# Gated delta net: a level's two independent tiled products in one burst, and tiled steps of two heads side by side

## The chip, the cores and the metric

The kernel runs on one core of a Trainium2 chip. The metric is the device time of one execution in microseconds (us); the kernel before is given by the median of three runs. The engines are PE (TensorE, matrix products), DVE (VectorE), ACT (ScalarE), POOL (GpSimd) and SP (SyncE, which issues transfers).

## The reference

A stack of four blocks over a sequence of 512 tokens of width 1024, in float32: a first block with a pooling mixer and a gated delta net, an MLP, a sparse attention block and a state space block. The change is in the gated delta net of the first block. It has 4 heads of width 128; the sequence is cut into 8 chunks of 64 tokens. Per head and chunk it computes

```python
kb = kh * beta[..., None]
m = jnp.einsum('bhncd,bhnjd->bhncj', kb, kh) * decay_strict
lhs = jnp.eye(C, dtype=f32) + m
rhs = jnp.concatenate([vh * beta[..., None], kb * jnp.exp(gcum)[..., None]], axis=-1)
sol = lax.linalg.triangular_solve(lhs, rhs, left_side=True, lower=True)
value, k_cumdecay = sol[..., :Dh], sol[..., Dh:]
attn_inner = jnp.einsum('bhncd,bhnjd->bhncj', qh, kh) * decay_incl
...
v_new = val - jnp.einsum('bhcd,bhde->bhce', kc, state)
o = jnp.einsum('bhcd,bhde->bhce', qd, state) + jnp.einsum('bhcj,bhje->bhce', ai, v_new)
state = state * jnp.exp(gl)[..., None, None] + jnp.einsum('bhcd,bhce->bhde', kd, v_new)
```

The step that matters here is the inverse of the 64x64 unit lower triangular `lhs`.

## The kernel before

**Two streams on PE.** In the first block PE has a main stream: dense products of 128x128 weights with 512 tokens, each float32 product made of three float32r matmuls (line 133, called L133 in the profile). They are the projections of `w_in` (20 tiles of 24 matmuls: keys, queries and values of heads 0 to 3, gates, pooling) and then `w_out`. Beside it run side streams, each a Python generator: `gdn_chain` for each head, `gdn_norm` behind it, `decays` once, `pooling` four times. A chain starts when its head's three convolutions are there and the head before it has passed level 4 (`mid`), so the end of one head overlaps with the start of the next: this text calls it a hand-over, of which there are three.

**The planner.** `weave` writes the order on PE. It keeps a clock `t` in estimated us. One step of the main stream is one dense matmul and counts 0.22. A side stream yields a pair after each step: what the step cost, and how long until its next step may run; the second figure is multiplied by `LATE` = 1.1. The side step with the earliest due time runs when it is due and nothing is owed; after a side step of cost c the main stream is owed 0.5 c, paid by dense matmuls. PE and SP follow this order to the letter (`manual_schedule(engines=MANUAL)`); DVE, ACT and POOL are ordered by the scheduler of the language, by priority (`RUSH` for side steps) and by what is ready in its model.

**The chain of a head.** Its products by line: `pk` (514, four transposes of the keys, from which POOL makes the squares `ksq` and DVE the norms `k2`, `rk2`, `brk2` and later `rk`), `pq` and `pn` (533 to 536, keys times keys and queries, the array split into two tiles of 128x64), `pd` (539, 540, decays), then six levels, 0 to 5, that build the inverse by doubling, then the join of two chunks (639 to 648), then `pz`, `pA`, `pc`, `po` and the pass over the states (`pS`, lines 685 to 691).

A level works on eight 64x64 matrices, four on partitions 0 to 63 and four on 64 to 127; a helper `each` issues eight products, each of which is two matmul instructions in the trace, on the array tiles at (0, 0) and (64, 64). These 64x64 products, and `pq` with `pn`, are called tiled here. Level n has
- `pb` (579): the level's mask of `M` (`Ms`, made by POOL) times `U`; ACT copies it to `B`.
- `px` (584, from level 2 on): the `B0` of the level before times `X`; DVE subtracts it from `X`.
- `pu` (588): `X` times `B`; DVE subtracts it from `U` (at level 5 into `UU`, line 595).

`px` does not depend on the `pb` of its level; `pu` needs both. Before the change the chain yields between each two of the three, so dense matmuls or another stream's steps stand between them. Behind level 1 there is a step `pv`, behind level 3 `pr`, behind level 4 `q2` (`token_sums`). The join at lines 639 and 640 issues a last `px` and a `pb` that reads `UU`, in one step already.

Banks of PSUM for the chain come from a pool of five.

Of the kernel before, what the change touches and what calls it, by code (L numbers as in the profile page):

```python
# [20 lines left out]
LATER = 4000  # L21
POOLED = (2, 3, 4, 5)
LATE = 1.1
SHARE = 0.5
BLOCKED = object()


def weave(tc, main, sides):

    t, owed, active = 0.0, 0.0, []
    while sides or active:
        for e in list(sides):
            if e[0]():
                sides.remove(e)
                active.append([t, e[1]])
        due = min(active, key=lambda e: e[0]) if active else None
        if due is None or due[0] > t or owed > 0.0:
            owed -= 0.22  # L40
            if next(main, BLOCKED) is BLOCKED:
                assert due is not None or any(e[0]() for e in sides)
                t, owed = max(t, due[0] if due else t), 0.0
            else:
                t += 0.22
            continue
        with tc.high_priority(RUSH):
            step = next(due[1], None)
        if step is None:
            active.remove(due)  # L50
        else:
            t += step[0]
            owed = max(owed, -0.22) + SHARE * step[0]
            due[0] = t + LATE * step[1]
    while next(main) is not BLOCKED:
        pass

# [10 lines left out]
class Kit:  # L68
# [217 lines left out]
    def bank(self):  # L286
        return self.norm_bank() if self.norm_bank else self.psd.tile([128, 512], F32, tag="ps", name="ps")
# [188 lines left out]
def gdn_chain(K, h, inputs, cst, G, gw, bank, result, mid):  # L476
# [14 lines left out]
    def bc(t, n):  # L491
        return t[:, :, None].to_broadcast([t.shape[0], 4, n])

    def each(f):
        for i in range(4):
            for x in range(2):
                f(i, halves[x], (x * 64, x * 64))

    def v4(t):
        return t.rearrange("p (i c) -> p i c", i=4)  # L500
# [23 lines left out]
    nc.vector.reciprocal(rk2, k2)  # L524
    brk2 = gw.tile([128, 4], F32, tag="brk2", name="brk2")
    nc.vector.tensor_tensor(brk2, rk2, beta, ALU.mult)
    yield 0.5, 0.0

    pq, pn = bank("pq"), bank("pn")
    for i in range(4):  # L530
# [29 lines left out]
    Mn = dec[:, 2]  # L560
    nc.vector.tensor_tensor(Mn[high], Mn[high], bc(brk2[high], 64), ALU.mult)
    nc.vector.tensor_tensor(Mn[high], v4(pn[high, 0:256]), Mn[high], ALU.mult)
    yield 0.9, 5.0


    foldb = fold[:, None, :].to_broadcast([128, 4, 64])
    for n in range(6):
        lev = cst[:, None, C_LEV + 64 * n:C_LEV + 64 * n + 64].to_broadcast([128, 4, 64])
        Ms = gw.tile([128, 4, 64], F32, tag="Ms", name="Ms", bufs=4)
        nc.gpsimd.tensor_tensor(Ms, M, lev, ALU.mult)  # L570
        pb = bank("pb")
        if n == 0:
            each(lambda i, s, tp: mm(pb[s, i * 64:i * 64 + 64], Ms[s, i, :], fold[s, :], start=True, stop=True, tile_position=tp))
            U, X = (gw.tile([128, 4, 64], F32, tag=t, name=t) for t in "UX")
            nc.vector.tensor_tensor(U, foldb, v4(pb[:, 0:256]), ALU.subtract)
            nc.gpsimd.tensor_tensor(X, foldb, Ms, ALU.subtract)
        else:
            B = gw.tile([128, 4, 64], F32, tag="B", name="B", bufs=3)
            each(lambda i, s, tp: mm(pb[s, i * 64:i * 64 + 64], Ms[s, i, :], U[s, i, :], start=True, stop=True, tile_position=tp))  # L579
            nc.scalar.copy(B, v4(pb[:, 0:256]))  # L580
            yield 0.6, 0.0
            if n > 1:
                px = bank("px")
                each(lambda i, s, tp: mm(px[s, i * 64:i * 64 + 64], B0[s, i, :], X[s, i, :], start=True, stop=True, tile_position=tp))
                nc.vector.tensor_tensor(X, X, v4(px[:, 0:256]), ALU.subtract)
                yield 0.6, 1.0
            pu = bank("pu")
            each(lambda i, s, tp: mm(pu[s, i * 64:i * 64 + 64], X[s, i, :], B[s, i, :], start=True, stop=True, tile_position=tp))
            if n < 5:
                nc.vector.tensor_tensor(U, U, v4(pu[:, 0:256]), ALU.subtract)  # L590
            else:
                UU = gw.tile([128, 4, 128], F32, tag="s2", name="UU", bufs=2)
                nc.gpsimd.memset(UU[high, :, 0:64], 0.0)
                for s in (high, low):
                    nc.vector.tensor_tensor(UU[s, :, s], U[s], v4(pu[s, 0:256]), ALU.subtract)
            B0 = B
        yield 0.6, 1.0
        if n == 1:

            pv = bank("pv")  # L600
            for i in range(4):
                nc.tensor.transpose(pv[:, i * 128:i * 128 + 128], vT[:, i * 128:i * 128 + 128], ident)
            rk = gw.tile([128, 4], F32, tag="rk", name="rk")
            K.rsqrt(rk, k2, "g")
            brke = gw.tile([128, 4], F32, tag="brke", name="brke")
            nc.vector.tensor_tensor(brke, brk2, eg, ALU.mult)
            brk = gw.tile([128, 4], F32, tag="brk", name="brk")
            nc.vector.tensor_tensor(brk, rk, beta, ALU.mult)
            R = gw.tile([128, 4, 256], F32, tag="R", name="R")
            nc.vector.tensor_tensor(R[:, :, 0:128], pv.rearrange("p (i d) -> p i d", i=4), bc(brk, 128), ALU.mult)  # L610
            nc.gpsimd.tensor_tensor(R[:, :, 128:256], kt, bc(brke, 128), ALU.mult)
            yield 0.5, 0.2
        if n == 2:
            kd = gw.tile([128, 4, 128], F32, tag="kd", name="kd")
            nc.gpsimd.tensor_tensor(kd, kt, bc(ekd, 128), ALU.mult)
        if n == 3:

            pr = bank("pr")
            for part, first in ((ghi, True), (glo, False)):
                d = gw.tile([128, 4, 128], F32R, tag="s2", name="gd", bufs=2)  # L620
                nc.gpsimd.tensor_tensor(d, ident[:, None, :].to_broadcast([128, 4, 128]), bc(part, 128), ALU.mult)
                mm(pr, G["ones"], d.rearrange("p i c -> p (i c)"), start=first, stop=not first)
            qc = gw.tile([128, 4, 128], F32, tag="kt", name="qc")
            qcf = qc.rearrange("p i c -> p (i c)")
            nc.scalar.activation(qcf, pr, AF.Exp)
            nc.gpsimd.tensor_tensor(qcf, qcf, kq[:, 1, :], ALU.mult)
            qq = gw.tile([128, 512], F32, tag="s2", name="gqq", bufs=2)
            nc.scalar.activation(qq, kq[:, 1, :], AF.Square)
            yield 0.9, 0.2
        if n == 4:  # L630
            mid.add(h)
            q2 = K.token_sums([(qq, K.ones[:, 0:1])], 128 * EPS, 128 * EPS * EPS, "gts", bank("pt"))
            yield 0.9, 0.0


    px, pb = bank("px"), bank("pb")
# [4 lines left out]
    nc.vector.tensor_tensor(X[low], X[low], v4(px[low, 0:256]), ALU.subtract)  # L641
    B = gw.tile([128, 4, 64], F32, tag="B", name="B", bufs=3)
    nc.scalar.copy(B[low], v4(pb[low, 0:256]))
    yield 0.6, 1.0
    pu = bank("pu")
    for i in range(4):
        mm(pu[low, i * 64:i * 64 + 64], X[low, i, :], B[low, i, :], start=True, stop=True, tile_position=(0, 0))
# [71 lines left out]
def block1(K, vec, wcol, W, V, mx, mixh, mixl, then):  # L719
# [5 lines left out]
    with tc.tile_pool(name="gq", bufs=1) as gq, tc.tile_pool(name="gw", bufs=2) as gw, \  # L725
# [209 lines left out]
        with tc.manual_schedule(engines=MANUAL):  # L935
            for done, ps in held:
                done(ps)
            sides.append((lambda: True, dc))
            for h in range(4):
                sides.append((lambda h=h: "gcum" in G and len(convs.get(h, ())) == 3 and (h < 2 or h - 2 in o) and (h < 1 or h - 1 in mid),  # L940
                              gdn_chain(K, h, inputs, cst, G, gw, bank, o, mid)))
                sides.append((lambda h=h: h in o and h in zs, gdn_norm(K, h, zs, o, V, gw, bank, mixh[4 + h], mixl[4 + h], mixed)))
            weave(tc, K.passes, sides)
# [27 lines left out]
def nsa(K, norms, W, cst, first, then):  # L971
# [12 lines left out]
    with ExitStack() as pools:  # L984
# [342 lines left out]
        def units():  # L1327
# [4 lines left out]
            for n in range(len(items) + LAGS[2]):  # L1332
                for stage, lag in enumerate(LAGS):
# [10 lines left out]
                    if n - lag < len(items):  # L1344
                        yield FILL[at[0]][at[1]] * 0.22 / SHARE / 3, 0.0

# [17 lines left out]
        with tc.manual_schedule(engines=MANUAL):  # L1364
            for c in range(2):
                p.memset(KD[c][:, :, 511:528], 0.0)
            p.memset(Vc, 0.0)
            K.norm_bank = lambda: bank("norm")
            K.lead(K.norm2_steps(*norms, R), R, held, 28, 42)
            K.norm_bank = None  # L1370
            weave(tc, K.passes, sides)
# [778 lines left out]
```

## Time and profile before

| | us |
|---|---|
| median of three runs | 1344.16 |
| lowest, highest | 1341.83, 1345.73 |
| profiled execution, its own time | 1345.95 |
| span of the profiled execution | 1343.8 |
| mean granted clock of TensorE in it | 0.983 |

The span runs from the first to the last instruction. The gated delta net lies between 40 and 260 us of it. A timeline row reads: start, length from the first start to the last end, engine, line, operation, output and inputs by the program's names, weight and operand shapes, count, and in brackets the idle time of the engine before it with its releaser. Matmuls overlap, so the pace is read from starts, not from lengths. A row of source gives minimum, median and maximum ns of one instruction, first and last start, and forms. A row of waits gives who waited for whom, us in total, times, and the longest. [...]

### The profile page before, as it was taken

The page shows a single profiled execution, that of the slowest core. Times are in us where ns is not written, and L with a number is a line of the kernel's source. Part 1 is how long each engine was busy: PE and PEld are TensorE (multiplying, and loading weights), DVE is VectorE, ACT ScalarE, POOL GpSimd, SP SyncE. Part 2 cuts the span into 40 slices and gives each one's busy share as a digit, 9 for nine tenths or more (in the row PEclk, how much of TensorE's full clock was granted, in tenths as well). Part 3 has the DMA queues.
Part 4 walks back from the last instruction along what each step waited for, and adds up shares of the span by engine and source line. Part 5 has one row for each costly group of instructions (what it writes and reads, how often), then busy time and mean ns, then how long its engine had stood idle before and what let it go on. Part 6 is the DMA issues. An engine that isn't in the chain of part 4 may idle for free.

```text
span 1343.8 us, 22524 instructions
## 1 busy us (share of the span) xinstructions
PE 1287.7 (96%) x8360; PEld 1040.8 (77%) x8360; DVE 935.3 (70%) x2163; ACT 547.7 (41%) x1167; POOL 413.6 (31%) x456
## 2 busy tenths in 40 slices
PE   8899998999998999999999999999999989999997
PEld 5677776887886888888888877887877777778896
DVE  7967785558979768768676667777886665634465
ACT  4233232334322333323424546665754513334364
POOL 4723442121015566654121003444553200003200
PEclk8899999999998999999999999999999989999998
DMA  5121101133342344434445855312005269833331
GB/s 193 32 64 32 33 32 44 48 126 100 95 142 74 132 147 144 150 132 169 152 125 161 205 159 140 83 60 78 18 18 188 83 196 286 238 95 110 94 110 63
DMA packets 81197, 152.94 MB, mean 114 GB/s; under 512 B 23840, under 2 KB 46000, under 8 KB 79936
## 3 DMA queue, kind: packets, MB, share of 16 engines
q1 hardware_dynamic: 71408, 130.46, 31.4%
q0 software_dynamic: 2688, 15.75, 3.6%
q10 hardware_dynamic: 6992, 5.30, 1.4%
q8 instruction: 66, 1.08, 0.3%
q14 instruction: 43, 0.35, 0.1%
HBM read 119.60 MB, written 21.40 MB: 105 GB/s over the span
## 4 chain that ended last, share of the span: by engine, by line
PE 75%; DVE 13%; DMA 4%; issue 3%; ACT 2%; POOL 2%; SPq 0%; DVEq 0%; ACTq 0%; POOLq 0%
PE ps L133 53%; PE ps L1887 3%; DVE lo L107 3%; PE pa L1207 2%; PE acc L1304 2%; PE pt L1265 2%; PE pv L1088 2%; DMA sq<-D 2%; DMA Uc<-D 1%; DVE xlbuf L238 1%; ACT P L1216 1%; PE py L1818 1%; PE pb L579 1%; DVE cacc L457 1%; PE hid L1120 1%
## 5 line engine op out<-in xcount | busy, mean ns | idle before, releaser
L106 ACT CAST hi<-raw 128x512 fp32r<-128x512 f32 x357 | 203.0, 612 | 337.2 <-PE ps L133 257.2
L107 DVE TENSOR_TENSOR lo<-raw,hi 128x512 fp32r<-128x512 f32 x357 | 276.0, 798 | 73.0 <-ACT hi L106 72.7
L133 PE MATMUL ps<-xlbuf,hi 128*128 128x512 f32 x736 | 303.3, 412 | 4.6 <-DVE xlbuf L238 4.6
L133 PE MATMUL ps<-xhbuf,hi 128*128 128x512 f32 x736 | 302.3, 411 | 4.8 <-ACT hi L106 3.7
L133 PE MATMUL ps<-xhbuf,lo 128*128 128x512 f32 x736 | 299.5, 407 | 3.3 <-DVE lo L107 3.3
L133 PEld LDWEIGHTS ps<-xhbuf,hi 128*128 128x128 f32 x736 | 140.6, 191 | 39.8 <-issue 6.8
L133 PEld LDWEIGHTS ps<-xlbuf,hi 128*128 128x128 f32 x736 | 140.7, 191 | 35.8 <-DVE xlbuf L238 7.5
L133 PEld LDWEIGHTS ps<-xhbuf,lo 128*128 128x128 f32 x736 | 140.8, 191 | 34.7 <-DVE lo L107 6.1
L1221 POOL TENSOR_TENSOR P<-P,sm 128x128 f32<-128x128 f32 (+3 forms) x128 | 96.2, 772 | 191.0 <-DVE sm L1219 139.6
L133 PE MATMUL ps<-hh,hi 128*128 128x512 f32 x256 | 100.5, 393 | 0.0
L133 PE MATMUL ps<-hl,hi 128*128 128x512 f32 x256 | 99.7, 390 | 0.0
L133 PE MATMUL ps<-hh,lo 128*128 128x512 f32 x256 | 99.7, 389 | 0.0
L1216 ACT ACTIVATE P<-P,nm 128x128 f32<-128x128 f32 (+3 forms) x128 | 71.8, 562 | 59.1 <-DVE nm L1215 49.6
L1215 DVE CUSTOM_DVE_ANT_0 P<-pa,nc 128x128 f32<-128x128 f32 (+3 forms) x128 | 60.2, 485 | 11.1 <-PE pa L1207 10.2
L1645 POOL TENSOR_TENSOR F<-keep 128x512 f32<-128x512 f32 x32 | 42.1, 1336 | 81.1 <-PE pt L1673 50.8
L133 PEld LDWEIGHTS ps<-hh,hi 128*128 128x128 f32 x256 | 48.1, 188 | 10.5 <-issue 0.8
L1645 POOL TENSOR_TENSOR V<-keep 128x576 f32<-128x576 f32 x32 | 44.9, 1421 | 36.1 <-DMA DM<-V 35.6
L133 PEld LDWEIGHTS ps<-hh,lo 128*128 128x128 f32 x256 | 48.1, 188 | 10.0
L133 PEld LDWEIGHTS ps<-hl,hi 128*128 128x128 f32 x256 | 48.1, 188 | 9.7
L1265 PE MATMUL pt<-ident,P 128*128 128x128 f32 x320 | 47.3, 275 | 3.8 <-POOL P L1221 1.7
L133 PE MATMUL ps<-yh,hi 128*128 128x512 f32 x128 | 50.0, 391 | 0.6 <-ACT hi L106 0.6
L133 PE MATMUL ps<-yh,lo 128*128 128x512 f32 x128 | 50.0, 391 | 0.0
(557 smaller groups left out, 2546.0 us busy)
## 6 DMA issues: line engine op xcount, KB each, us to landing
raw<-in_wup_dram SPq DMA_DIRECT2D x32, 512.0 KB, 3.5
raw<-in_wdown_dram SPq DMA_DIRECT2D x32, 512.0 KB, 3.5
made<-DM POOLq DMA_DIRECT2D x8, 1472.0 KB, 9.0
raw<-in_win_dram SPq DMA_DIRECT2D x19, 512.0 KB, 3.5
raw<-in_s_wglu_dram SPq DMA_DIRECT2D x16, 512.0 KB, 3.5
DM<-V SPq DMA_DIRECT2D x8, 576.0 KB, 3.0
DM<-Wt SPq DMA_DIRECT2D x8, 512.0 KB, 2.9
raw<-in_n_kv_dram SPq DMA_DIRECT2D x8, 512.0 KB, 3.9
```

Source lines behind the costliest of these rows:

```text
L106: self.nc.scalar.copy(hi[:, s], raw[:, s])
L107: self.nc.vector.tensor_tensor(lo[:, s], raw[:, s], hi[:, s].bitcast(F32), ALU.subtract)
L133: mm(ps, w[:, s], xs[k][x], start=k == 0 and n == 0, stop=k == kt - 1 and n == 2)
L1088: mm(R["v"][i], x[k][:, i * 128:i * 128 + 128], w[:, s], start=k == 0 and n == 0, stop=k == 7 and n == 2)
L1207: mm(pa[g2][:, 0:lead + nk], QS[gp][:, g2, i, r, :], keys[b][:, gp * 2 + g2, key0:AT[b] + nk], start=n == 0, stop=n == 1)
L1215: v.tensor_tensor_reduce(P[g2][:, 0:nk], pa[g2][:, lead:lead + nk], pos[:, 512 - nk:512], -slope, 3e38, ALU.add, ALU.min, nm[:, g2:g2 + 1])
L1216: act.activation(P[g2][:, 0:nk], P[g2][:, 0:nk], AF.Exp, scale=-1.0, bias=nm[:, g2:g2 + 1], accum_out=sm[:, g2:g2 + 1])
L1221: p.tensor_tensor(P[g2][:, 0:nk], P[g2][:, 0:nk], sm[:, g2:g2 + 1].to_broadcast([128, nk]), ALU.mult)
L1265: nc.tensor.transpose(pt[:, s], P[g2][:, s], ident)
L1304: mm(o[halves[g2], q * 128:q * 128 + 128], Vt[:, j, c:c + 64], T[g2][:, s], start=fresh and (q, j) == (0, 0), stop=(b, q, j) == (1, 3, i), ...
L1645: eng.tensor_tensor(o[:, x:x + 4], self.S[f][:, js, b * 8 + x:b * 8 + x + 4].rearrange("p j x -> p x j")[:, :, :, None].to_broadcast([128, ...
L1887: nc.tensor.matmul(banks[m][:, 0:256], w[:, s], os[k][x][:, a * 256:a * 256 + 256], start=k == 0 and n == 0, stop=k == 7 and n == 2)
```

## The change

A side stream can now mark that its next step is tiled, by a third element in what it yields. `weave` keeps this mark for each active stream and remembers in `tiled` whether the last thing it placed was a tiled side step. Three rules follow. If the last step was tiled and another tiled step is due, that one is taken next, the earliest due first, whatever is owed to the main stream. If the step to be taken is tiled and does not follow a tiled one, it waits while another stream's tiled step comes due within `HOLD` = 0.7. Any dense matmul resets `tiled`.

In `gdn_chain` the yield between `pb` and `px` goes, so levels 2 to 5 issue both in one step of cost 1.2, followed by the due time of 1.0 x 1.1; at level 1, which has no `px`, the yield behind `pb` now has that due time too, where it was 0. All other changed lines only add the mark. No instruction is added or removed.

```diff
--- before.py
+++ after.py
@@ -21,6 +21,7 @@
 LATER = 4000
 POOLED = (2, 3, 4, 5)
 LATE = 1.1
+HOLD = 0.7
 SHARE = 0.5
 BLOCKED = object()
 
@@ -29,21 +30,29 @@
 
 
 
-    t, owed, active = 0.0, 0.0, []
+
+    t, owed, active, tiled = 0.0, 0.0, [], False
     while sides or active:
         for e in list(sides):
             if e[0]():
                 sides.remove(e)
-                active.append([t, e[1]])
+                active.append([t, e[1], False])
         due = min(active, key=lambda e: e[0]) if active else None
-        if due is None or due[0] > t or owed > 0.0:
+        wait = due is None or due[0] > t
+        if not wait and tiled:
+            due = min((e for e in active if e[2] and e[0] <= t), key=lambda e: e[0], default=due)
+        if not wait and not (tiled and due[2]):
+            wait = owed > 0.0 or due[2] and any(e[2] and t < e[0] <= t + HOLD for e in active)
+        if wait:
             owed -= 0.22
+            tiled = False
             if next(main, BLOCKED) is BLOCKED:
                 assert due is not None or any(e[0]() for e in sides)
                 t, owed = max(t, due[0] if due else t), 0.0
             else:
                 t += 0.22
             continue
+        tiled = due[2]
         with tc.high_priority(RUSH):
             step = next(due[1], None)
         if step is None:
@@ -51,7 +60,7 @@
         else:
             t += step[0]
             owed = max(owed, -0.22) + SHARE * step[0]
-            due[0] = t + LATE * step[1]
+            due[0], due[2] = t + LATE * step[1], len(step) > 2
     while next(main) is not BLOCKED:
         pass
 
@@ -524,7 +533,7 @@
     nc.vector.reciprocal(rk2, k2)
     brk2 = gw.tile([128, 4], F32, tag="brk2", name="brk2")
     nc.vector.tensor_tensor(brk2, rk2, beta, ALU.mult)
-    yield 0.5, 0.0
+    yield 0.5, 0.0, True
 
     pq, pn = bank("pq"), bank("pn")
     for i in range(4):
@@ -560,7 +569,7 @@
     Mn = dec[:, 2]
     nc.vector.tensor_tensor(Mn[high], Mn[high], bc(brk2[high], 64), ALU.mult)
     nc.vector.tensor_tensor(Mn[high], v4(pn[high, 0:256]), Mn[high], ALU.mult)
-    yield 0.9, 5.0
+    yield 0.9, 5.0, True
 
 
     foldb = fold[:, None, :].to_broadcast([128, 4, 64])
@@ -578,12 +587,11 @@
             B = gw.tile([128, 4, 64], F32, tag="B", name="B", bufs=3)
             each(lambda i, s, tp: mm(pb[s, i * 64:i * 64 + 64], Ms[s, i, :], U[s, i, :], start=True, stop=True, tile_position=tp))
             nc.scalar.copy(B, v4(pb[:, 0:256]))
-            yield 0.6, 0.0
             if n > 1:
                 px = bank("px")
                 each(lambda i, s, tp: mm(px[s, i * 64:i * 64 + 64], B0[s, i, :], X[s, i, :], start=True, stop=True, tile_position=tp))
                 nc.vector.tensor_tensor(X, X, v4(px[:, 0:256]), ALU.subtract)
-                yield 0.6, 1.0
+            yield 0.6 if n == 1 else 1.2, 1.0, True
             pu = bank("pu")
             each(lambda i, s, tp: mm(pu[s, i * 64:i * 64 + 64], X[s, i, :], B[s, i, :], start=True, stop=True, tile_position=tp))
             if n < 5:
@@ -594,7 +602,8 @@
                 for s in (high, low):
                     nc.vector.tensor_tensor(UU[s, :, s], U[s], v4(pu[s, 0:256]), ALU.subtract)
             B0 = B
-        yield 0.6, 1.0
+
+        yield (0.6, 1.0) if n in (1, 3, 4) else (0.6, 1.0, True)
         if n == 1:
 
             pv = bank("pv")
@@ -609,7 +618,7 @@
             R = gw.tile([128, 4, 256], F32, tag="R", name="R")
             nc.vector.tensor_tensor(R[:, :, 0:128], pv.rearrange("p (i d) -> p i d", i=4), bc(brk, 128), ALU.mult)
             nc.gpsimd.tensor_tensor(R[:, :, 128:256], kt, bc(brke, 128), ALU.mult)
-            yield 0.5, 0.2
+            yield 0.5, 0.2, True
         if n == 2:
             kd = gw.tile([128, 4, 128], F32, tag="kd", name="kd")
             nc.gpsimd.tensor_tensor(kd, kt, bc(ekd, 128), ALU.mult)
@@ -626,11 +635,11 @@
             nc.gpsimd.tensor_tensor(qcf, qcf, kq[:, 1, :], ALU.mult)
             qq = gw.tile([128, 512], F32, tag="s2", name="gqq", bufs=2)
             nc.scalar.activation(qq, kq[:, 1, :], AF.Square)
-            yield 0.9, 0.2
+            yield 0.9, 0.2, True
         if n == 4:
             mid.add(h)
             q2 = K.token_sums([(qq, K.ones[:, 0:1])], 128 * EPS, 128 * EPS * EPS, "gts", bank("pt"))
-            yield 0.9, 0.0
+            yield 0.9, 0.0, True
 
 
     px, pb = bank("px"), bank("pb")
@@ -641,7 +650,7 @@
     nc.vector.tensor_tensor(X[low], X[low], v4(px[low, 0:256]), ALU.subtract)
     B = gw.tile([128, 4, 64], F32, tag="B", name="B", bufs=3)
     nc.scalar.copy(B[low], v4(pb[low, 0:256]))
-    yield 0.6, 1.0
+    yield 0.6, 1.0, True
     pu = bank("pu")
     for i in range(4):
         mm(pu[low, i * 64:i * 64 + 64], X[low, i, :], B[low, i, :], start=True, stop=True, tile_position=(0, 0))
```

## Rows read from the trace of the kernel before

**Rows 1.** The page: the span, and busy time of each engine

```profile
span 1343.8 us, 22524 instructions
...
PE 1287.7 (96%) x8360; PEld 1040.8 (77%) x8360; DVE 935.3 (70%) x2163; ACT 547.7 (41%) x1167; POOL 413.6 (31%) x456
```

**Rows 2.** Windows of 20 us, 40 to 300 us, and their sum

```profile
60.00:80.00 20.00, 18.32 (x174) 13.22 (x171) 15.83 (x32) 6.05 (x12) 6.29 (x10) 0.84 0.16 54
...
140.00:160.00 20.00, 17.43 (x145) 13.18 (x144) 18.08 (x42) 4.97 (x10) 9.26 (x11) 0.91 0.18 53
...
sum 260.00, PE 242.88 PEld 188.85 DVE 180.46 ACT 81.29 POOL 89.13; mean PE 18.68 PEld 14.53 DVE 13.88 ACT 6.25 POOL 6.86
```

**Rows 3.** Source line 584: all matmuls of `px`

```profile
L584 PE MATMUL px<-X,B x256: 218/218/267, 71.4 to 232.5; 64*64 64x64 f32 x128
```

**Rows 4.** Timeline of PE, a level of the first head

```profile
75.45 0.39 PE L133 MATMUL ps<-xhbuf,lo 128*128 128x512 f32 x1
75.76 0.68 PE L579 MATMUL pb<-U,Ms 64*64 64x64 f32 x16
76.38 0.51 PE L133 MATMUL ps<-xhbuf,hi 128*128 128x512 f32 x1
76.81 0.68 PE L584 MATMUL px<-X,B 64*64 64x64 f32 x16
77.42 0.51 PE L133 MATMUL ps<-xlbuf,hi 128*128 128x512 f32 x1
77.77 0.40 PE L133 MATMUL ps<-xhbuf,lo 128*128 128x512 f32 x1
78.00 0.40 PE L133 MATMUL ps<-xhbuf,hi 128*128 128x512 f32 x1
```

**Rows 5.** Timeline of PE, first row of `pq`, first row behind `pn`

```profile
137.98 0.44 PE L533 MATMUL pq<-kq 128*64 128x128 f32 x4
...
139.47 0.50 PE L133 MATMUL ps<-xlbuf,hi 128*128 128x512 f32 x1
```

**Rows 6.** Waits of PE, 43 to 260 us: first and last of 13 rows, and one between

```profile
PE pb L579 <- DVE U L575: 2.4, 2, 1.5
...
PE pb L640 <- DVE rk L281: 1.7, 1, 1.7
...
PE pu L647 <- DVE X L641: 0.3, 1, 0.3
```

**Rows 7.** Timeline of PE, first and third hand-over between heads

```profile
89.90 0.60 PE L514 MATMUL pk<-ident,kq 128*128 128x128 f32 x4
...
96.69 0.32 PE L639 MATMUL px<-X,B 64*64 64x64 f32 x2
97.72 0.24 PE L640 MATMUL pb<-UU,dec 64*64 64x64 f32 x1 [0.71 <-DVE UU L595]
...
183.32 0.60 PE L514 MATMUL pk<-ident,kq 128*128 128x128 f32 x4
183.67 0.47 PE L133 MATMUL ps<-xhbuf,hi 128*128 128x512 f32 x1
...
188.92 0.60 PE L539 MATMUL pd<-gm,cst 128*128 128x256 f32 x2
...
190.01 0.40 PE L133 MATMUL ps<-xhbuf,hi 128*128 128x512 f32 x1
190.34 0.33 PE L639 MATMUL px<-X,B 64*64 64x64 f32 x2
191.06 0.24 PE L640 MATMUL pb<-UU,dec 64*64 64x64 f32 x1 [0.40 <-DVE brke L606]
```

**Rows 8.** Timeline of DVE, the same two hand-overs

```profile
96.72 0.85 DVE L595 TENSOR_TENSOR UU<-U,pu 64x256 f32<-64x256 f32 x2
...
185.69 0.69 DVE L520 TENSOR_REDUCE k<-ksq 128x4 f32<-128x512 f32 x1 [0.46 <-POOL ksq L518]
...
190.07 0.85 DVE L595 TENSOR_TENSOR UU<-U,pu 64x256 f32<-64x256 f32 x2
```

## The prediction

> **What bounds the kernel now.** I read the page first, then the stage that holds the gated delta net, and inside it PE alone. The page says that PE is busy for 96% of the span [rows 1], so what is taken from PE shows in the time unless something else then keeps PE waiting. The windows over the stage (40 to 300 us) give 242.9 us of PE work in 260, so 17.1 us of idle PE, and a granted clock under 1.00 in some stretches: 0.84 in 60 to 80 us, 0.91 in 140 to 160 us [rows 2]. The stage is therefore two things at once: a stream of full 128x128 dense matmuls with chain steps set in between, which PE works off without a gap, and some dozen places where PE stands before a chain step and waits, mostly for DVE. The view of PE's waits has thirteen rows there, 17.1 us in all [rows 6]. The change touches both: it makes the first kind of time shorter, and it moves steps around the second.
>
> PE's order is the program's, so the planner `weave` sets it. I followed its clock through the step costs in the code; the order it gives for the kernel before is the order of the trace (one dense matmul between `pb` and `px`, as in [rows 4]). The same arithmetic with the changed rules gives the new order used below.
>
> **What a tiled burst costs.** Each of the 16 bursts of `px` (256 matmuls, 16 a burst) [rows 3] stands one dense matmul, seldom a few steps, behind its `pb`. In the steady stretch from 75.45 to 77.77 us there are three dense matmuls and two bursts [rows 4]. A dense matmul follows a dense matmul after 0.23 us (77.77 to 78.00). So two bursts cost 2.32 - 3 x 0.23 = 1.63 us, 0.81 us each. The work inside is less: a burst's row is 0.68 us long, its last matmul takes 0.218 us [rows 3], so 15 spacings are 0.46 us and one is 0.031 us; 16 matmuls are 0.49 us of PE. The remaining 0.32 us lie at the edges: the burst starts 0.31 instead of 0.23 us after the dense matmul, the dense one behind it starts 0.61 instead of 0.49 us after the burst's first, and the next dense one 0.35 us after that (77.42 to 77.77).
>
> **Part one, `pb` and `px` in one burst.** No instruction is added or removed, and no DMA; the yield between the two products goes. Levels 2 to 5 of four heads make 16 mergers. The second product then costs its 16 spacings, 0.49 us, in place of 0.81: 16 x 0.32 = 5.1 us less PE time. Lower end: the one burst of 32 matmuls in the trace (`pq` with `pn`) takes 1.49 us with its way out, 0.047 us a matmul [rows 5]; at that spacing the second product costs 0.75 us, a merger gives 0.06 us, and all of them 1.0 us. Half of that burst's matmuls have 128 columns, so it is the further row; I take 0.32. Upper end: the first merger falls where PE ran at half clock, so perhaps 0.3 us more.
>
> Does the merger make anything late? `px` needs `B0` and `X`, both made a level earlier. Between `px` and `pu` there stay five or six dense matmuls (or steps of another head), so DVE's subtraction into `X` keeps its cover of 1.2 to 1.4 us; ACT's copy into `B` loses some 0.56 us (1.05 from `pb`'s start to `px`'s in [rows 4], less 0.49) but is needed only at `pu`. I cost both at nothing; without that cover each level would wait some tenths. At level 1 the yield is now followed by 1.1 of planned wait: for the first head `pu` moves behind six dense matmuls instead of one, which only reorders PE.
>
> **Part two, tiled steps that meet.** After a tiled step the planner now takes any other tiled step that is due, whatever is owed to the dense stream, and holds one back up to 0.7 for another. Followed through: after level 5's burst of a head, `pk` of the next head (cost 0.5) and one dense matmul bring the planner past the due times of both `pq` (next head) and `pu` (this head), so they run together. That happens at the first and second hand-over; at the third it is `pu`, `pq`, and the next `px`+`pb` (line 639) in a row. In all 72 separate tiled groups become 52: 16 by the mergers and 4 by meetings. Two 64x64 bursts of different heads never meet without a `pq` between them. `pq` is 128x64 and the others 64x64, and no row shows such a change of shape. Bounds: nothing (it costs like any switch) to 0.32 us each (it is free). A change of shape is nearest to the edges in [rows 4], which cost 0.08 us on the way in and 0.24 us on the way out; I take half of the pair, 0.15 us, 0.6 us in all.
>
> [...]
>
> **Waits.** What is saved shortly before a wait for DVE is lost in it, because DVE does not arrive earlier. At five waits for `X` or for line 640's `UU` (the longest 1.7 us [rows 6]) one or two mergers lie in the few microseconds ahead: about five mergers, 1.6 us lost. Against that, at the first two hand-overs `pu` now stands four and three dense matmuls further from `px`+`pb` (0.9 and 0.7 us), so the waits there (1.0 us from 96.69 to 97.72 [rows 7]; 1.7 us in [rows 6]) should shrink; as `pk` has come nearer too, I count 0.9 us of the 1.6. Net 0.7 us lost.
>
> **Sum.** 5.1 + 0.6 - 0.7 = 5.0 us. The profiled execution took 1345.95 us (span 1343.8); it becomes 1340.95, and the stages behind are not touched: the dense stream goes on from the same place, earlier. Against the median of 1344.16, 1.8 us lower, that is 1339.2 us.
>
> **Rivals.**
> *DVE eats most of it* (no change that can be measured; for this kernel that means within 0.3%, 4.0 us). DVE's queue is ordered anew, and its bursts of work after each convolution keep their length. If nine mergers end in waits (2.9 us) and the third hand-over waits a microsecond more, 5.7 - 3.9 = 1.8 us remain: 1342.4. For it: the thirteen waits; against it: between them PE runs for 10 us and more without one.
>
> *`UU` stays behind the next head's work on DVE* (slower). Line 640 needs `UU`, which DVE makes after `pu`. Today DVE finishes it 97.57 - 89.90 = 7.7 us after the next head's `pk` at the first hand-over and 190.92 - 183.32 = 7.6 us at the third [rows 7, 8], because that head's norm chain is ahead of it in DVE's queue. In the new order only `pk` (0.35), two dense (0.47), `pu` with its way in (0.08 + 0.49) and `pq` (1.49) stand between `pk` and line 639 at the third: 2.9 us. If DVE's order stays, PE waits 4.7 us instead of 0.7 (190.34 to 191.06). At the first: `pk`, six dense (1.4) and `pq`, `pu` as above, `pd` with two dense (1.09 + 0.23) plus 0.2 of edges, 5.3 us, so 2.4 instead of 1.0. That adds 5.4 us. [...] Against it: `pu` could end 1.4 us after `pk` by the same terms, while the norm chain's first DVE instruction starts 2.4 us after it (185.69 [rows 8]); a queue ordered by what is ready puts `UU` first.
>
> *Long runs of tiled matmuls slow down* (little change). [...] The meetings make runs of 48, 48 and 64: 64 matmuls beyond 32. At 0.047 instead of 0.031 us they cost 1.0 us and the meetings then give nothing: 1339.2 + 1.6 = 1340.8, and with a lower price of the mergers too (0.047 for the last 8 of each, 2.0 us) 1342.8. [...]
>
> *The hand-over waits vanish*, with the dip to 0.91 behind the second: 1.7 + 1.0 + 1.8 us, of which 0.9 is in the sum already: 1335.6.
>
> **Chances.** Forecast 0.54; waits vanish 0.07; DVE eats it 0.20; long runs slow 0.09 (half of it still beyond 4.0 us); `UU` late 0.10. Faster by over 0.3%: 0.54 less a tenth of it that ends short of 4.0 us, plus 0.07, plus 0.04: 0.60. Slower: the `UU` case in full, 0.08. Rest 0.32. The likeliest's own range is 1336.5 to 1341.5; the 8-in-10 range goes down to 1333, past the vanished waits with the upper ends of both parts, and up to 1346, the `UU` case in half.
>
> **What would show it.** Right: `px` starting 0.03 us after the last `pb`, no L133 row between; a pair of them 1.10 us from first matmul to next dense; 52 tiled groups; the sum of PE's waits between 40 and 260 us within 2 us of 17.1. Meetings: the first `pu` behind `pn` after 0.03 us (free) or 0.1 and more (a switch). Wrong: a wait above 3 us at line 640 with wide matmuls at 0.43 us behind it; or spacings above 0.04 us in the second half of a burst; or a DVE wait grown behind each merger.

## The result, and the profile after

The changed kernel takes 1337.82 us (median; 1334.03 to 1339.38), the one before 1344.16: a ratio of 0.9949 (95% interval 0.9932 to 0.9967), 6.3 us faster. Forecast were 1339.2 us, faster. Intervals of ratios leave out two single executions, of 5049.39 us (the kernel before) and 1578.91 us (mergers only, below).

Line numbers of the changed kernel are 9 or 10 higher (L133 is L142, L579 is L588, L584 is L592, L588 is L596, L640 is L649). PE's timeline of one level of the first head, as in [rows 4]:

```profile
75.32 0.39 PE L142 MATMUL ps<-xhbuf,hi 128*128 128x512 f32 x1
75.64 0.68 PE L588 MATMUL pb<-U,Ms 64*64 64x64 f32 x16
76.15 0.63 PE L592 MATMUL px<-X,B 64*64 64x64 f32 x16
76.71 0.50 PE L142 MATMUL ps<-xlbuf,hi 128*128 128x512 f32 x1
77.05 0.39 PE L142 MATMUL ps<-xhbuf,lo 128*128 128x512 f32 x1
77.28 0.40 PE L142 MATMUL ps<-xhbuf,hi 128*128 128x512 f32 x1
```

`px` follows `pb` without a dense matmul between. The timeline has 52 separate tiled groups where it had 72. From 75.32 to 77.05 stand two dense matmuls and both products: 1.73 - 2 x 0.23 = 1.27 us, where it was 1.63. A merger gives 0.36 us.

The meetings, at the first and the third hand-over (timeline of PE, as in [rows 7]):

```profile
91.40 0.22 PE L545 MATMUL pn<-kq 128*64 128x64 f32 x1
91.56 0.68 PE L596 MATMUL pu<-B,X 64*64 64x64 f32 x16
92.17 0.50 PE L142 MATMUL ps<-xhbuf,lo 128*128 128x512 f32 x1
...
94.86 0.32 PE L648 MATMUL px<-X,B 64*64 64x64 f32 x2
95.93 0.24 PE L649 MATMUL pb<-UU,dec 64*64 64x64 f32 x1 [0.75 <-DVE yi L284]
...
176.30 0.68 PE L596 MATMUL pu<-B,X 64*64 64x64 f32 x16
176.91 0.44 PE L542 MATMUL pq<-kq 128*64 128x128 f32 x4
...
178.40 0.33 PE L648 MATMUL px<-X,B 64*64 64x64 f32 x2
180.09 0.24 PE L649 MATMUL pb<-UU,dec 64*64 64x64 f32 x1 [1.36 <-DVE UU L603]
```

`pu` starts 0.16 us after the last `pn`, not 0.03: the change from 128x64 to 64x64 costs 0.13 us, about the way out of a burst (0.12 in [rows 4]). What a meeting then saves is one way in (0.08) and one late dense matmul (0.12), 0.2 us by these rows, an estimate. The first hand-over waits as long as before (1.07 us from 94.86 to 95.93; 1.03 in [rows 7]); the third waits 1.69 us (178.40 to 180.09) instead of 0.72.

The waits of PE, 43 to 260 us, as in [rows 6], all of them:

```profile
PE pb L588 <- DVE t L289: 3.0, 1, 3.0
PE pg L849 <- POOL xp L461: 2.2, 1, 2.2
PE pu L656 <- ACT B L652: 2.0, 2, 1.3
PE pu L656 <- DVE pp L883: 2.0, 1, 2.0
PE pb L582 <- POOL Ms L579: 1.9, 1, 1.9
PE pb L588 <- DVE U L584: 1.5, 1, 1.5
PE pb L649 <- DVE UU L603: 1.4, 1, 1.4
PE pb L588 <- DVE rk L290: 1.3, 1, 1.3
PE pu L596 <- DVE t L289: 1.2, 1, 1.2
PE pb L649 <- DVE yi L284: 0.8, 1, 0.8
PE pz L665 <- DVE UU L657: 0.7, 1, 0.7
PE pu L596 <- DVE t L288: 0.6, 1, 0.6
PE pu L596 <- DVE y L290: 0.6, 1, 0.6
```

They are 19.2 us, 2.1 more than before, and in part they are other waits: the 1.7 us before line 640 of the second hand-over are gone, the 2.0 us before the last head's `pu` (L656) are new. The instruction that a row names is the last that DVE had finished, not always the one that PE needs: the 3.0 us at 64.22 ended 0.15 us after `U` (L584, 63.65 to 64.07), though the row names `t`. The granted clock moved too, to 0.91 from 0.84 in 60 to 80 us and to 1.00 from 0.91 in 140 to 160. A row of windows gives the stretch, its length, busy time with the number of instructions for PE, its weight loads (PEld), DVE, ACT and POOL, then the granted clock as a share of the full one, the DMA share and GB/s; the first two stretches are those of [rows 2]:

```profile
60.00:80.00 20.00, 17.00 (x174) 12.69 (x173) 16.77 (x34) 6.63 (x12) 5.86 (x9) 0.91 0.19 54
...
140.00:160.00 20.00, 18.70 (x181) 15.05 (x182) 15.07 (x32) 5.84 (x13) 8.29 (x11) 1.00 0.09 28
...
220.00:240.00 20.00, 18.02 (x131) 14.24 (x128) 9.54 (x16) 5.28 (x10) 6.94 (x8) 0.91 0.08 20
```

**An account of the stage.** The last addition of the first block's output projection is a mark behind all that was touched. In the source view of its line (before, then after) it starts at 305.6 and at 299.1 us:

```profile
L906 DVE TENSOR_TENSOR hbuf<-hbuf,ps x16: 675/686/689, 263.6 to 305.6; 128x512 f32<-128x512 f32 x16
```

```profile
L915 DVE TENSOR_TENSOR hbuf<-hbuf,ps x16: 674/687/689, 257.1 to 299.1; 128x512 f32<-128x512 f32 x16
```

So the stage gives 6.5 us. Between kernels this mark says more than the whole time: the rest behind it took between 1032 and 1042 us in the profiles of this study, in no relation to the kernel (the changed one alone: 1036.7, 1040.9 and 1038.1), while the mark of one kernel repeats within 1.3 us. From the mark I take off the time in which PE was not busy and what the lower clock cost, 20 x (1 - clock), both summed over windows of 20 us from 0 to the mark. What is left is an estimate of PE's own work, up to a constant. In kernels profiled more than once it repeats within 1.1 us:

| kernel | mark | idle | clock | work | ratio to before (interval) |
|---|---|---|---|---|---|
| before | 305.6 | 22.3 | 10.2 | 273.1 | 1 |
| changed | 299.1 | 23.9 | 8.8 | 266.4 | 0.9949 (0.9932 to 0.9967) |
| changed, again | 299.0 | 23.2 | 8.8 | 267.0 | 0.9936 (0.9913 to 0.9960) |
| changed, third | 299.6 | 23.2 | 10.4 | 266.0 | 0.9953 (0.9930 to 0.9975) |
| mergers only | 299.7 | 20.9 | 12.0 | 266.8 | 0.9940 (0.9915 to 0.9965) |
| mergers only, again | 299.7 | 20.6 | 12.0 | 267.1 | 0.9925 (0.9901 to 0.9950) |
| meetings only | 306.6 | 24.1 | 8.6 | 273.9 | 0.9996 (0.9977 to 1.0014) |
| `pu` split | 315.6 | 25.1 | 12.2 | 278.3 | 1.0099 (1.0072 to 1.0126) |
| changed, `px` first | 297.8 | 21.3 | 10.6 | 265.9 | 0.9942 (0.9921 to 0.9963) |
| mergers, `px` first | 293.1 | 18.3 | 7.0 | 267.8 | 0.9893 (0.9874 to 0.9912) |
| mergers, `px` first, again | 294.4 | 17.3 | 10.4 | 266.7 | 0.9889 (0.9867 to 0.9912) |
| changed, third apart | 296.7 | 21.3 | 8.8 | 266.6 | 0.9929 (0.9911 to 0.9946) |
| changed, `pA` `pc` `po` in one | 295.2 | 18.8 | 10.4 | 266.0 | 0.9907 (0.9889 to 0.9926) |
| combined | 294.4 | 18.7 | 8.6 | 267.1 | 0.9894 (0.9868 to 0.9919) |

Waits and clock belong together. Level 1's `pb` of the first head starts 5.25 us after level 0's before (59.39 to 64.64) and 5.26 us after it changed (58.96 to 64.22). Changed, PE stood 3.00 us ahead of it, at a granted clock of 1.00 over that stretch; before, 1.55 us, at 0.67, where the dense matmuls between followed each other after 0.43 us instead of 0.23 and filled the wait. In the two profiles of mergers with `px` first the longest wait of a `pb` (L583) for DVE is 3.0 and 1.7 us, with 7.0 and 10.4 us of clock in the table.

A part of the whole gain is the clock's, an estimate from the median granted clock of each kernel's executions: (1 - clock) x span was 20.8 us before and 16.7 changed on one chip, 21.5 and 20.0 on another, 4.1 and 1.5 us less out of 7.2 and 5.9 us.

### The profile page after: what moved, and what is told of

It is laid out like the page before. It is cut to its first block, busy times and chain, and to the rows that moved or that the text cites. A ratio compares the mean times of both kernels' runs of the same rounds, so it can differ in the third digit from the quotient of the medians.

```text
span 1335.8 us, 22532 instructions
## 1 busy us (share of the span) xinstructions
PE 1278.5 (96%) x8360; PEld 1038.2 (78%) x8360; DVE 933.4 (70%) x2163; ACT 547.7 (41%) x1167; POOL 414.4 (31%) x456
## 4 chain that ended last, share of the span: by engine, by line
PE 76%; DVE 14%; issue 3%; ACT 2%; DMA 2%; POOL 2%; SPq 0%; DVEq 0%; ACTq 0%; POOLq 0%
PE ps L142 54%; PE ps L1896 3%; PE pa L1216 2%; DVE lo L116 2%; PE acc L1313 2%; PE pt L1274 2%; PE pv L1097 2%; DVE cacc L466 1%; PE py L1827 1%; DVE xlbuf L247 1%; ACT P L1225 1%; PE hid L1129 1%; PE pb L588 1%; DMA T<-DK 1%; PE py L1820 1%
## 5 line engine op out<-in xcount | busy, mean ns | idle before, releaser
L142 PE MATMUL ps<-xhbuf,hi 128*128 128x512 f32 x736 | 302.1, 410 | 4.7 <-ACT hi L115 3.7
L142 PE MATMUL ps<-xlbuf,hi 128*128 128x512 f32 x736 | 301.2, 409 | 4.3 <-DVE xlbuf L247 4.1
L142 PE MATMUL ps<-xhbuf,lo 128*128 128x512 f32 x736 | 297.7, 404 | 3.8 <-DVE lo L116 3.8
L142 PEld LDWEIGHTS ps<-xhbuf,hi 128*128 128x128 f32 x736 | 140.2, 190 | 39.1 <-ACT hi L115 6.2
L142 PEld LDWEIGHTS ps<-xlbuf,hi 128*128 128x128 f32 x736 | 140.5, 191 | 35.1 <-DVE xlbuf L247 7.4
L142 PEld LDWEIGHTS ps<-xhbuf,lo 128*128 128x128 f32 x736 | 140.1, 190 | 35.5 <-DVE lo L116 6.6
L142 PE MATMUL ps<-hh,hi 128*128 128x512 f32 x256 | 100.6, 393 | 0.0
L142 PE MATMUL ps<-hl,hi 128*128 128x512 f32 x256 | 99.8, 390 | 0.0
L142 PE MATMUL ps<-hh,lo 128*128 128x512 f32 x256 | 99.7, 390 | 0.0
L142 PEld LDWEIGHTS ps<-hh,hi 128*128 128x128 f32 x256 | 48.1, 188 | 10.5 <-issue 0.8
L142 PEld LDWEIGHTS ps<-hh,lo 128*128 128x128 f32 x256 | 48.1, 188 | 10.0
L142 PEld LDWEIGHTS ps<-hl,hi 128*128 128x128 f32 x256 | 48.1, 188 | 9.7
L398 DVE TENSOR_TENSOR hbuf<-hbuf,ps 128x512 f32<-128x512 f32 x32 | 21.9, 686 | 41.7 <-PE ps L142 41.6
L142 PE MATMUL ps<-yh,lo 128*128 128x512 f32 x128 | 50.1, 391 | 0.3 <-DVE lo L116 0.3
```

The costliest lines, as they stand in the source:

```text
L142: mm(ps, w[:, s], xs[k][x], start=k == 0 and n == 0, stop=k == kt - 1 and n == 2)
```

## The experiments

The theory: PE loses an edge around each tiled burst, and 20 edges less are the gain. The rival: the gain comes from the order of the work on DVE, that is, from the waits. The experiments ran on three chips, each with the kernel before beside them; across chips the ratios of the table are compared.

**Changed kernel again** (as it is, the measure for the next three).

> The changed kernel once more, as the measure for the three others on the same chip. Theory (the edges of tiled bursts): 6 us below the kernel before, the last addition of the output projection in the first block 6.5 us earlier than before (305.6 us in the profile before). Rival (order of the work on DVE): the same sum, but a different split of it between edges and waits.

Measured 1338.01 us, mark at 299.0.

**Mergers only.** On the kernel before:

```diff
             nc.scalar.copy(B, v4(pb[:, 0:256]))
-            yield 0.6, 0.0
...
-                yield 0.6, 1.0
+            yield 0.6 if n == 1 else 1.2, 1.0
             pu = bank("pu")
```

> The planner of the kernel before, with the yield between pb and px taken out: 16 mergers, no meetings, 56 tiled groups. Theory: 16 x 0.36 = 5.8 us less PE time, waits about as in the changed kernel, so 5 to 6 us below the kernel before and within 1.5 us of the changed one. Rival (the gain comes from where steps meet at the hand-overs and from the order on DVE): under 3 us.

Measured 1336.55 us; by the account 6.3 us less work than before, and 6.0 in a second profile. Its mark is 5.9 us earlier, as expected; by the ratio of times it is 8 us under the kernel before (4.7 to 11.4). The mergers alone do what the change does.

**Meetings only.** On the changed kernel:

```diff
             nc.scalar.copy(B, v4(pb[:, 0:256]))
+            yield 0.6, 0.0
...
-            yield 0.6 if n == 1 else 1.2, 1.0, True
+                yield 0.6, 1.0, True
```

> The changed planner and the marks, but pb and px keep a yield between them and the px step is not marked: by the planner's arithmetic three meetings, each of pq with pu, 69 tiled groups. Theory: 3 x 0.2 = 0.6 us less PE time, so within 2 us of the kernel before, waits deciding the sign. Rival: 3 us or more below it.

Measured 1343.55 us against 1345.23 for the kernel before on that chip: no change that can be told. Its work comes out 0.8 us above before where 0.6 below was expected; that difference is not explained, and shows about how far the account can be trusted.

**`pu` split.** On the kernel before, `each` with a range:

```diff
-            each(lambda i, s, tp: mm(pu[...], X[s, i, :], B[s, i, :], ...))
+            each(lambda i, s, tp: mm(pu[...], X[s, i, :], B[s, i, :], ...), 0, 2)
+            if n < 5:
+                K.run(1)
+            each(lambda i, s, tp: mm(pu[...], X[s, i, :], B[s, i, :], ...), 2, 4)
```

> The kernel before with 16 more edges: at levels 1 to 4 of each head pu is issued in two halves of 8 matmuls with one dense matmul between them. No instruction is added. Theory: each split costs an edge of 0.32 to 0.36 us, 5.1 to 5.8 us slower than the kernel before in all, waits aside. Rival (an edge is hidden or is part of the tiled work itself): within 2 us of the kernel before.

Measured 1358.92 us, 13.7 above the kernel before on that chip (1345.23); mark at 315.6, 10.0 us later. The other 3.7 us are not split up here; the median granted clock over the whole span is 0.9795, against 0.9845 before. One split in PE's timeline:

```profile
73.19 0.40 PE L133 MATMUL ps<-xhbuf,hi 128*128 128x512 f32 x1
73.52 0.45 PE L588 MATMUL pu<-B,X 64*64 64x64 f32 x8
73.90 0.49 PE L133 MATMUL ps<-xlbuf,hi 128*128 128x512 f32 x1
74.32 0.45 PE L591 MATMUL pu<-B,X 64*64 64x64 f32 x8
74.70 0.50 PE L133 MATMUL ps<-xhbuf,lo 128*128 128x512 f32 x1
75.04 0.39 PE L133 MATMUL ps<-xhbuf,hi 128*128 128x512 f32 x1
```

From 73.19 to 75.04 there are three dense matmuls and one burst of 16: 1.85 - 0.69 = 1.16 us, 0.35 more than the 0.81 of an unsplit one. 16 x 0.35 = 5.6 us; the account gives 5.2 us of work, 2.8 of idle time and 2.0 of clock. The edge has its price in both directions; idle time and clock come on top.

**`px` first.** In the merged step, on the changed kernel and on mergers only, the `px` block moves ahead of `pb` and its copy:

```diff
+            if n > 1:
+                px = bank("px")
+                each(lambda i, s, tp: mm(px[...], B0[s, i, :], X[s, i, :], ...))
+                nc.vector.tensor_tensor(X, X, v4(px[:, 0:256]), ALU.subtract)
             each(lambda i, s, tp: mm(pb[...], Ms[s, i, :], U[s, i, :], ...))
             nc.scalar.copy(B, v4(pb[:, 0:256]))
```

> The changed kernel with px ahead of pb inside the merged burst. px needs nothing of this level, so PE can do its 0.5 us while U is still on its way, and DVE gets px's result 0.5 us earlier. Theory (the edges are paid off, what is left are waits for DVE): edges unchanged, the three waits of pu for X (2.4 us) and those of pb for U shrink by up to 2 us together; 0 to 2 us below the changed kernel. Rival (DVE's order, not the arrival of its inputs, sets these waits): no difference.

> The mergers without the meetings (planner of the kernel before), with px ahead of pb. Theory: as the kernel with mergers alone, less up to 2 us of waits; 1334 to 1338 us. Rival: like the kernel with mergers alone.

> Mergers alone, beside the changed kernel and the one with px first on one chip. Theory (the meetings give nothing net: their edges of 0.2 us go into longer waits): at or up to 3 us below the changed kernel. Rival (meetings help): 1 us or more above it.

> Mergers alone with px first. If putting px first is what made 1329.05 us of it, 3 us or more below mergers alone; if it was the lower clock falling elsewhere in those executions, within 2 us of mergers alone.

Measured with the meetings 1338.25 us; without them 1329.05 and, on another chip, 1331.65 beside 1336.60 for mergers only and 1339.27 for the changed kernel. The work is the same within its repeats; on mergers only the sum of idle time and clock falls by 5 to 8 us. The three waits of `pu` for `X` (1.2, 0.6 and 0.6 us) are gone in both. A part is the clock's, how large is not settled: on the chip that ran both mergers only and `px` first on them, where the time fell by 4.9 us, (1 - clock) x span falls by the estimate from medians from 20.7 to 16.0 us, in the stage of the two profiled executions only from 12.0 to 10.4. Beside the meetings idle time falls as well (21.3 for 23.2 to 23.9) but the clock does not rise (median 0.984, with 0.9855 for the kernel before on that chip), and by its ratio the kernel is level with the changed one. The first two expectations saw at most 2 us of waits in it and had no term for the clock. Why the clock rises in the one order and not in the other, no run shows.

**Third hand-over apart.**

```diff
-        yield (0.6, 1.0) if n in (1, 3, 4) else (0.6, 1.0, True)
+        yield (0.6, 1.0) if n in (1, 3, 4, 5) else (0.6, 1.0, True)
```

> The changed kernel, with the mark taken from the step of lines 648 and 649 only: by the planner's arithmetic five dense matmuls stand between pq and that step at the third hand-over, the rest of the order is the same. Theory: the wait of 1.4 us there (1.7 us from the burst's start to its third matmul) falls under 0.6 us, one edge of about 0.2 us comes back, 0 to 1 us below the changed kernel. Rival (UU is late by the queue on DVE, wherever PE stands): the wait stays above 1 us.

Measured 1334.58 us, mark 2.4 us earlier than in the changed kernel, more than the 0 to 1 expected; the intervals of the two ratios overlap, so the time alone does not tell them apart. PE's timeline there:

```profile
178.32 0.50 PE L142 MATMUL ps<-xhbuf,hi 128*128 128x512 f32 x1
...
179.67 0.33 PE L648 MATMUL px<-X,B 64*64 64x64 f32 x2
180.01 0.24 PE L649 MATMUL pb<-UU,dec 64*64 64x64 f32 x1
```

Five dense matmuls now fill the time that PE stood, and 0.34 us are left of the 1.69. The triple meeting paid 1.35 us of waiting for one edge. The 1.5 us of line 588 behind it (at 194.02 in the changed kernel) are gone as well.

**`pA`, `pc`, `po` in one step.** Two yields out, the third with the sum of the costs:

```diff
     nc.vector.tensor_tensor(AT, AT, pA..., ALU.subtract)
-    yield 0.9, 0.0
...
     nc.vector.tensor_tensor(qc, qc, pc..., ALU.subtract)
-    yield 0.9, 0.0
...
-    yield 0.9, 0.0
+    yield 2.7, 0.0
```

> The changed kernel with the three steps pA, pc and po of each head issued as one step: 24 full 128x128 matmuls of 128 columns in a row instead of three times 8, eight edges of short full matmuls less. If an edge is only the change of the array's tile shape, nothing is saved here (0 us). If half or more of it is that short matmuls beside long ones leave weight loads uncovered (0.2 us an edge by the four transposes pt in the profile before), 8 x 0.2 = 1.6 us less PE time, waits aside.

Measured 1331.37 us. PE's timeline:

```profile
105.25 0.39 PE L142 MATMUL ps<-xhbuf,lo 128*128 128x512 f32 x1
105.48 1.05 PE L674 MATMUL pA<-kd,R 128*128 128x128 f32 x8
106.37 1.06 PE L680 MATMUL pc<-at,R 128*128 128x128 f32 x8
107.26 1.06 PE L686 MATMUL po<-R,at 128*128 128x128 f32 x8
108.07 0.47 PE L142 MATMUL ps<-xhbuf,hi 128*128 128x512 f32 x1
108.39 0.39 PE L142 MATMUL ps<-xlbuf,hi 128*128 128x512 f32 x1
```

3.14 - 2 x 0.23 = 2.68 us for three, 0.89 each. In the changed kernel `pA` stands alone between dense matmuls:

```profile
104.67 0.39 PE L142 MATMUL ps<-xhbuf,lo 128*128 128x512 f32 x1
104.90 1.05 PE L674 MATMUL pA<-kd,R 128*128 128x128 f32 x8
105.71 0.48 PE L142 MATMUL ps<-xhbuf,hi 128*128 128x512 f32 x1
106.03 0.39 PE L142 MATMUL ps<-xlbuf,hi 128*128 128x512 f32 x1
```

1.36 - 0.46 = 0.90 us. These 128x128 matmuls have no edge to save; the bursts of another tile shape have one. The kernel is faster all the same, with the same work: PE's idle time is 18.8 us for 23.9, of which the clock takes 1.6 back. Here the rival's mechanism works without the theory's.

**Combined**: mergers only, `px` first, `pA` `pc` `po` in one step.

> The planner of the kernel before, no marks; px and pb in one step with px first; pA, pc and po of a head in one step. Theory: 16 edges of tiled bursts less (5.8 us), no edge saved among the full matmuls (as measured: three steps in a row cost three times one), but fewer waits for DVE, as in the kernel with that one step: 1325 to 1331 us. Rival (the two effects on waits are the same one): like the mergers with px first, 1329 to 1331.

> The changed kernel as the measure for the three others: 5 to 8 us below the kernel before.

Measured 1331.73 us, level with mergers and `px` first (1331.65), as the rival had it. The two effects on waits don't add; by its ratio no version was faster than mergers with `px` first, 7.6 us under the changed kernel on the same chip.

## Why the prediction was right

**The mergers** carried it, as said. 5.1 us were forecast and 6.0 to 6.3 measured on mergers only: the edge was sized 0.32 us and is 0.36 (1.27 us for the pair instead of 1.63; 16 make 5.8), since a pair takes 1.07 us to the next dense matmul where 1.10 was worked out. The doubled edge agrees (0.35 each). The 0.3 us more at the upper end had no ground: the first merger's place (70.33 to 71.98 us before) had a granted clock of 1.00 (70 to 72 us), behind 0.50 in 68 to 70.

**The meetings** were sized 0.6 us; the work of the changed kernel lies about 0.5 us under that of the mergers, less than the account's own scatter. And mergers only is not slower than the changed kernel (1336.55 to 1338.01, 1336.60 to 1339.27), so no net gain of the meetings shows. A change from 128x64 to 64x64 has its price too: `pu` at 91.56 comes after 0.16 us. No edge stood where the shape stayed the same (`px` starts 0.51 us after `pb` at 75.64, 16 spacings of 0.03).

**The waits** were put at 0.7 us lost. The list of PE's waits grew by 2.1 us, just past the 2 us that the prediction allowed itself; three waits of `pu` for `X`, a lateness that it cost at nothing, are 2.4 us of the list and were 1.7. In the table idle time grew by 1.6 us, and the clock, for which the sum had no term, gave 1.4 back. So without the clock the account has 6.7 - 1.6 = 5.1 us for the forecast 5.0: a larger saving of work and a larger loss in waits. That the two cancel is luck, and so is that waits and clock together come near the 0.7 us lost: in the other two profiles of the changed kernel idle time and clock add up to 32.0 and 33.6 us (32.5 before).

The first hand-over did not shrink (1.07 us for 1.03): `pu` stands 0.9 us further from line 640, but `pk` 1.2 us nearer, and on DVE `UU` still came behind that head's `k` (L531, 93.67 to 94.68). The second did (nothing over 0.3 us before L649), but 1.3 us came back before `pu` at L656. The third grew by 1.0 us, in part by the rival that `UU` stays behind the next head's work. L649 reads one half of `UU`; it starts 0.15 us after the first of the two in the timeline ends (179.94). That half came behind 0.67 us of the next head's `k` and 1.50 us of an earlier head's norm (`ml`):

```profile
177.38 1.50 DVE L244 TENSOR_TENSOR ml<-z,mh 128x512 fp32r<-128x512 f32 x1
178.81 0.67 DVE L529 TENSOR_REDUCE k<-ksq 128x4 f32<-128x512 f32 x1
179.52 0.42 DVE L603 TENSOR_TENSOR UU<-U,pu 64x256 f32<-64x256 f32 x1
179.97 0.89 DVE L531 TENSOR_SCALAR k<-k 128x4 f32<-128x4 f32 x1
180.90 0.41 DVE L603 TENSOR_TENSOR UU<-U,pu 64x256 f32<-64x256 f32 x1
```

The chance of slower and the upper end of 1346 us took for the `UU` case a loss of clock behind its waits, on top of its 5.4 us. No run shows that term as it was counted; in the changed kernel the granted clock stayed at 1.00 behind the 1.07 and the 1.69 us at L649 (94 to 102 and 178 to 188 us).

Not foreseen was the wait of 2.0 us at L656: `X` (L650) came on DVE behind a step of the pooling (`pp`), which itself waited for POOL until 226.75.

**Long runs of tiled matmuls** don't slow down: in the run of 64 at the third hand-over `pu` still takes 0.61 us and `pq` with `pn` 1.49.

Open: why the clock falls behind some waits and not others (behind 1.83 us at L573 it was 0.50 in 60 to 62 us before, behind 1.88 us at L582 it was 1.00 there in the changed kernel); by that, why `px` first gives 5 us without the meetings and next to nothing with them.

## What to carry to other kernels

Count the changes of tile shape on PE, not the tiled work: a pair of them, into a burst and out, cost 0.36 us here, and independent products of one shape belong in one burst, the one whose operands come first ahead. A rule that draws steps of different chains together needs the result of the step to be there: a wait 1 us longer undid several edges. Where waits for another engine are as large as the gain, the order of steps is worth as much as the work saved, partly through the clock (`px` first took 5 to 8 us of idle time and clock off mergers only), and has to be measured.

## What the runs showed of the hardware

Some tiny DVE instructions lasted until a long one of POOL beside them ended. In the changed kernel one on 128x4 numbers took 1.21 us (the median of L289 is 0.16), to 126.47, POOL's `qc` to 126.45:

```profile
125.26 1.21 DVE L289 SCALAR_TENSOR_TENSOR t<-gv,t 128x4 f32<-128x4 f32 x1
```

```profile
125.16 1.29 POOL L635 TENSOR_TENSOR qc<-qc,kq 128x512 f32<-128x512 f32 x1 [0.38 <-ACT qc L634]
...
179.79 1.05 POOL L630 TENSOR_TENSOR gd<-ident,ghi 128x512 fp32r<-128x512 f32 x1
```

It happens again at 213.72, where L289 took 1.17 us (to 214.89, POOL's `qc` to 214.87), and in every head at L531 (`k`, 128x4), 0.77 to 1.01 us: at 179.97 it ends at 180.86, POOL's `gd` at 180.84. Why they end together, no run shows. Two of these stand on PE's path: the `X` that `pu` waits for at 215.76 came behind the L289 of 213.72, and `UU` at the first hand-over behind `k`. It is one source of DVE's lateness; whether another order would avoid the overlap, no run shows.
